# A gated linear-recurrence decoder step on one core: one score matmul per block, two-part sums of squares, and VectorE transposes

## The chip, the cores and the metric

The kernel is one program on one core of a Trainium2 chip. Its inputs are laid out by the host beforehand, and it is launched once. The metric is the device time of one execution in microseconds (us). Before the change three runs took 1477.56, 1477.69 and 1478.64 us, so the median is 1477.69 us.

The engines are named as the profile names them: PE is the matrix engine (PEld its weight loads), DVE is VectorE, ACT is ScalarE, POOL is GpSimd and SP is the engine that issues nearly all DMAs here.

## The reference

264 columns of activations are worked on together: 256 tokens of one prompt and 8 single-token samples. Everything is float32, with a model width of 2048.

```
hx    = rmsnorm(x) ; proj = hx @ w_in            # 11264 outputs: 88 blocks of 128
u     = cg * hc ; a = bg * conv3(u)              # short-convolution branch
f     = lb + (1-lb)*sigmoid(fz) ; log_f = log f ; k = 1-f
b     = cumsum(log_f) inside a chunk of 64 tokens
o     = tril((q e^b) @ (k e^-b)^T) @ v  +  (q e^b) @ S_start       # per head
S_end = e^{b_last} * S_start + (k e^{b_last-b})^T @ v
o     = rmsnorm(o) * silu(og)                    # norm over 128 channels of a head
x     = x + (sig(ga)*(a@w_a) + sig(gb)*(o@w_b)) @ w_out
y     = rmsnorm(x + relu(rmsnorm(x) @ w_up)^2 @ w_down)
```

The prompt's recurrence is exact per token, whatever the chunk length. A sample takes one step of the recurrence with its own stored state, `S = f*S + k v^T`, `o = S^T q`, and returns the new state.

## The kernel before, in words

**Layout.** Channels lie on the 128 partitions and the 264 columns on the free axis. Each large product is made of blocks of 128 output channels. A block's weights (1 MB) come in one DMA (`fetch_w`, L72 to L77). They are split in two halves into a high part `whi` (rounded to fp32r by ACT, L65) and a low remainder `wlo` (DVE, L66). PE adds three fp32r products per tile of 128 input channels, `whi*xh`, `whi*xl` and `wlo*xh` (`gemm`, L90 to L96). A block of 16 tiles is therefore 48 passes over 264 columns.

**Buffers.** There are two raw weight buffers, four buffers for split halves, five PSUM buffers `acc` for the products and three PSUM buffers `mps` for everything small.

**The projection loop** (L538 to L573) has 56 slots, and its order is written out by hand on every engine. In slot i the program first issues the fetch for slot i+2, then evacuates the product of slot i-1 (L508, times `rstd1`), then splits the weights of slot i+1, then runs the steps that are due (`todo`), and then PE does the product of slot i, followed by the small PE work that is due (`todo_pe`). Each engine works through its own instructions strictly in this order. SP's fetch waits until the raw buffer is free, that is until the `wlo` of two slots earlier has been made.

**The recurrence** is done for two heads at a time, a pair; there are four pairs. The 15 steps `s0` to `s14` of a pair (`hgrn`, L252) follow the evacuation of its last block, one per slot. Pairs are evacuated in slots 4, 16, 28 and 40, so step 12 of one pair falls in the slot of step 0 of the next, and step 14 in that of step 2. The steps that matter here:

- `s0` and `s1`: sigmoid and log on ACT (different activation tables, each loaded before use), and `gs`, the 32 columns of factors `f` and `q` for the samples, collected by POOL. PE transposes `gs` at the end of slot 1.
- `s2`: ACT copies the transposed factors to `gsT` (L286), SP writes them to DRAM scratch `scr` (L288), DVE makes the cumulative sum `b`.
- `s3`: SP loads the samples' states `so` and broadcasts the factors from `scr` to all partitions as `fb` and `qb`, six DMAs of 512 KB for a pair (L322 to L324).
- `s4`, `s5`: products with exponentials; PE transposes of `v` and `kend`; ACT copies the transposes to `vk` (L363).
- `sco(i)` (L366 to L382) on PE: for head 0 at the end of slot 5, for head 1 at the end of slot 6. With chunks of 64 inside blocks of 128, it needs two score matmuls within chunks, two 64x64 score matmuls across the two chunks of a block, and two matmuls for the state increments, in two PSUM buffers.
- `s10` to `s13`: squares of `o`, their sum over partitions by a matmul with ones in plain float32 (L433), then log, exp and the products with the gate.

A plain float32 matmul is two passes on PE in the trace; an fp32r one is one.

**The column norms** `rstd1` and `rstd2` sum 16 blocks of squares elementwise, then use three tiny matmuls (`sumsq`), `rstd_diag` on 88x3 values, and a broadcast matmul (L133 to L137). For `rstd1` this is done while PE is in the first product, with the broadcast between its two halves (L551 to L553).

Outside the projection loop the order is set by a scheduler.

## Time and profile before

| what | value |
|---|---|
| median of three runs | 1477.69 us |
| the profiled execution's own time | 1477.44 us |
| its span (first to last instruction) | 1475.7 us |
| granted PE clock, mean | 0.997 |
| PE busy | 1463.1 us, 99% |
| DVE busy | 881.9 us, 60% |
| ACT busy | 707.4 us, 48% |
| POOL busy | 56.5 us, 4% |
| DMA | 285.90 MB, 194 GB/s mean |
| the projection loop with its head | about 29 to 379 us of the span |

The views used are the page with busy times and the chain of waits, the list of groups of instructions, the waits of an engine, the timeline of an engine (start, duration, engine, line, operation, tiles written and read, shapes, count; in brackets the idle time before and what ended it) and the table of windows (busy time of each engine, the granted clock, the share of time in which the 16 DMA engines worked, and GB/s). PE's passes overlap in the records, so what a pass costs is read from the distance between two starts and not from its own duration.

### The profile page before, as it was taken

The page shows a single profiled execution, that of the slowest core. Times are in us where ns is not written, and L with a number is a line of the kernel's source. Part 1 is how long each engine was busy: PE and PEld are TensorE (multiplying, and loading weights), DVE is VectorE, ACT ScalarE, POOL GpSimd, SP SyncE. Part 2 cuts the span into 40 slices and gives each one's busy share as a digit, 9 for nine tenths or more (in the row PEclk, how much of TensorE's full clock was granted, in tenths as well). Part 3 has the DMA queues.
Part 4 walks back from the last instruction along what each step waited for, and adds up shares of the span by engine and source line. Part 5 has one row for each costly group of instructions (what it writes and reads, how often), then busy time and mean ns, then how long its engine had stood idle before and what let it go on. Part 6 is the DMA issues. An engine that isn't in the chain of part 4 may idle for free.

```text
span 1475.7 us, 28089 instructions
## 1 busy us (share of the span) xinstructions
PE 1463.1 (99%) x12158; PEld 1460.0 (99%) x12158; DVE 881.9 (60%) x1154; ACT 707.4 (48%) x953; POOL 56.5 (4%) x87
## 2 busy tenths in 40 slices
PE   9999999999999999999999999999999999999997
PEld 9999999999999999999999999999999999999996
DVE  7667777777655555566655545555455554555554
ACT  7556565665444444444554433444334443344552
POOL 1001011012000000011100000000000000000000
PEclk9999999999999999999999999999999999999998
DMA  7575757575654555555555555455554555545541
GB/s 276 198 256 182 264 187 259 196 260 203 230 195 175 185 187 175 194 197 208 201 172 189 183 177 195 173 190 181 179 193 173 192 179 179 193 173 194 177 171 60
DMA packets 47388, 285.90 MB, mean 194 GB/s; under 512 B 5344, under 2 KB 9200, under 8 KB 16032
## 3 DMA queue, kind: packets, MB, share of 16 engines
q1 hardware_dynamic: 46848, 283.53, 54.1%
q8 instruction: 95, 1.56, 0.4%
q10 hardware_dynamic: 288, 0.40, 0.1%
q14 instruction: 29, 0.24, 0.0%
q0 software_dynamic: 128, 0.19, 0.0%
HBM read 277.07 MB, written 7.02 MB: 193 GB/s over the span
## 4 chain that ended last, share of the span: by engine, by line
PE 98%; DVE 1%; ACT 0%; issue 0%; DVEq 0%; ACTq 0%
PE proj L94 11%; PE proj L95 11%; PE proj L96 11%; PE dn L95 9%; PE up L95 9%; PE up L96 8%; PE dn L96 8%; PE up L94 8%; PE dn L94 8%; PE wo L94 2%; PE wo L95 2%; PE wo L96 2%; PE hd L157 2%; PE wps L112 0%; PE dlps L382 0%; DVE wlo L66 0%
## 5 line engine op out<-in xcount | busy, mean ns | idle before, releaser
L65 ACT CAST whi<-w 128x1024 fp32r<-128x1024 f32 x488 | 508.9, 1048 | 682.6 <-PE dn L95 212.7
L66 DVE TENSOR_TENSOR wlo<-w,whi 128x1024 fp32r<-128x1024 f32 x488 | 597.7, 1234 | 357.4 <-ACT whi L65 355.4
L94 PE MATMUL proj<-xgh,whi 128*128 128x264 f32 x1344 | 384.0, 286 | 0.4 <-DVE q L508 0.4
L95 PE MATMUL proj<-xgl,whi 128*128 128x264 f32 x1344 | 379.4, 282 | 0.0
L96 PE MATMUL proj<-xgh,wlo 128*128 128x264 f32 x1344 | 376.7, 280 | 0.0
L95 PE MATMUL dn<-hl,whi 128*128 128x264 f32 x1024 | 291.8, 285 | 0.0
L95 PE MATMUL up<-x2l,whi 128*128 128x264 f32 x1024 | 291.8, 285 | 0.0
L96 PE MATMUL dn<-hh,wlo 128*128 128x264 f32 x1024 | 289.3, 283 | 0.0
L96 PE MATMUL up<-x2h,wlo 128*128 128x264 f32 x1024 | 289.3, 282 | 0.0
L94 PE MATMUL up<-x2h,whi 128*128 128x264 f32 x1024 | 286.1, 279 | 0.0
L94 PE MATMUL dn<-hh,whi 128*128 128x264 f32 x1024 | 285.8, 279 | 0.0
L94 PEld LDWEIGHTS proj<-xgh,whi 128*128 128x128 f32 x1344 | 251.7, 187 | 0.8 <-ACT whi L65 0.6
L95 PEld LDWEIGHTS proj<-xgl,whi 128*128 128x128 f32 x1344 | 252.2, 188 | 0.2
L96 PEld LDWEIGHTS proj<-xgh,wlo 128*128 128x128 f32 x1344 | 252.3, 188 | 0.0
L94 PEld LDWEIGHTS up<-x2h,whi 128*128 128x128 f32 x1024 | 192.5, 188 | 0.0
L94 PEld LDWEIGHTS dn<-hh,whi 128*128 128x128 f32 x1024 | 192.5, 188 | 0.0
L96 PEld LDWEIGHTS up<-x2h,wlo 128*128 128x128 f32 x1024 | 192.3, 188 | 0.0
L96 PEld LDWEIGHTS dn<-hh,wlo 128*128 128x128 f32 x1024 | 192.3, 188 | 0.0
L95 PEld LDWEIGHTS up<-x2l,whi 128*128 128x128 f32 x1024 | 191.5, 187 | 0.0
L95 PEld LDWEIGHTS dn<-hl,whi 128*128 128x128 f32 x1024 | 191.5, 187 | 0.0
L94 PE MATMUL wo<-mxh,whi 128*128 128x264 f32 x256 | 73.0, 285 | 0.0
L95 PE MATMUL wo<-mxl,whi 128*128 128x264 f32 x256 | 72.3, 283 | 0.0
(405 smaller groups left out, 1304.2 us busy)
## 6 DMA issues: line engine op xcount, KB each, us to landing
w<-in_w_in_dram SPq DMA_DIRECT2D x84, 1024.0 KB, 4.8
w<-in_w_up_dram SPq DMA_DIRECT2D x64, 1024.0 KB, 4.7
w<-in_w_dn_dram SPq DMA_DIRECT2D x64, 1024.0 KB, 4.7
w<-in_w_br_dram SPq DMA_DIRECT2D x16, 1024.0 KB, 4.8
w<-in_w_out_dram SPq DMA_DIRECT2D x16, 1024.0 KB, 4.7
so<-in_shg_dram SPq DMA_DIRECT2D x8, 512.0 KB, 7.4
fb<-scr SPq DMA_DIRECT2D x8, 512.0 KB, 8.3
qb<-scr SPq DMA_DIRECT2D x8, 512.0 KB, 9.4
```

The lines of the kernel that those rows point to most:

```text
L65: nc.scalar.copy(hi, src)
L66: nc.vector.tensor_tensor(lo, src, hi.bitcast(F32), op=ALU.subtract)
L94: nc.tensor.matmul(ps, wh, xh, start=(k == 0), stop=False)
L95: nc.tensor.matmul(ps, wh, xl, start=False, stop=False)
L96: nc.tensor.matmul(ps, wl, xh, start=False, stop=(k == n - 1))
L157: nc.tensor.matmul(hps[i], a[:, i * P:(i + 1) * P], b, start=st, stop=sp)
```

## The change

Five edits go together.

1. **One score matmul per block.** The decay is taken relative to the middle of a block of 128 (`kin`, `qmid`), so one causal matmul of 128x128 covers a block. The two 64x64 matmuls, the ACT copy of their result, and the chunk bookkeeping go. Step 3 has four exponentials still, one of half the size.
2. **Both heads' scores and increments in one place.** `sco(0)` and `sco(1)` both run at the end of slot 5, each in one PSUM buffer, and `sta(0)` and `sta(1)` both in step 6.
3. **Two-part sums of squares.** Squares are split into two fp32r parts and summed by two fp32r matmuls with a 128x128 matrix of ones, which leaves the sum on every partition. For the heads' norms the squares move to steps 9 and 10, the matmuls to the end of step 11, and the steps after them move back by one (`s11` to `s14` run in slots 12 to 15).
4. **The column norms** use the same two matmuls (`rstd_all`), placed after the first product. `rstd` is then computed on 128x264 values, and no broadcast or copy follows. One of the four head accumulators moves from `acc` to `mps`.
5. **Sample factors transposed by VectorE.** Step 1 loses its PE transpose and step 2 its ACT copy; DVE transposes 32x32 blocks, and SP writes them to scratch in four DMAs.

```diff
-    def rstd_diag(ps, n, name):
...
-        r = const.tile([NB, 3], F32, name="r_" + name)
-        nc.vector.tensor_scalar(r, ps[:NB, 0:3], 1.0 / n, EPS, op0=ALU.mult, op1=ALU.add)
+    def ss_parts(ss, name):
+        parts = [tmp.tile([P, T], F32R, tag="t", name=f"{name}_{p}") for p in ("hi", "lo")]
+        split(ss, *parts)
+        return parts
+
+    def rstd_all(parts, n, name):
+
+        ps = mps.tile([P, 512], F32, tag="m", name="ps_" + name)[:, :T]
+        for p in range(2):
+            nc.tensor.matmul(ps, ones_r, parts[p], start=(p == 0), stop=(p == 1))
+        r = const.tile([P, T], F32, tag="rstd", name=name)
+        nc.vector.tensor_scalar(r, ps, 1.0 / n, EPS, op0=ALU.mult, op1=ALU.add)
         nc.vector.reciprocal(r, r)
         nc.scalar.activation(r, r, AF.Sqrt)
...
-    hps = [acc_tile(f"hd{i}") for i in range(4)]
+    hps = [acc_tile(f"hd{i}") for i in range(3)] + [mps.tile([P, 512], F32, tag="m", name="hd3")[:, :T]]
...
-        def s1p():
-            st["gsps"] = mps.tile([P, 512], F32, tag="m", name="gsps")
-            nc.tensor.transpose(out=st["gsps"][:32, :P], in_=st["gs"].rearrange("p a b c -> p (a b c)"),
-                                identity=ident)
-
         def s2():
-            gsT = hp.tile([32, P], F32, tag="gsT", name="gsT")
-            nc.scalar.copy(gsT, st["gsps"][:32, :P])
+
+            gsT = hp.tile([P, 32], F32, tag="gsT", name="gsT")
+            nc.vector.transpose(out=gsT, in_=st["gs"].rearrange("p a b c -> p (a b c)"))
             scr = st["scr"] = dram.tile([2, 2, TS, P], F32, name=f"scr{j}")
-            nc.sync.dma_start(scr.rearrange("a b c d -> (a b c) d"), gsT)
+            for c in range(4):
+                nc.sync.dma_start(scr.rearrange("a b c d -> (a b c) d")[:, 32 * c:32 * c + 32],
+                                  gsT[32 * c:32 * c + 32])
...
+            for dst, at in ((st["kend"], P - 1), (st["kin"], CH - 1)):
+                nc.vector.tensor_tensor(dst, b3[:, :, at:at + 1].broadcast_to([P, 4, P]), b3, op=ALU.subtract)
...
         def sco(i):
             ps = mps.tile([P, 512], F32, tag="m", name="scps")
+            p3 = ps.rearrange("p (a c) -> p a c", c=P)
+            st["scps", i], st["dl", i] = p3[:, 0:2], p3[:, 2:4]
             for blk in range(2):
-                r = slice(blk * P, (blk + 1) * P)
-                qb = qin[:, i, 2 * blk:2 * blk + 2].rearrange("p c l -> p (c l)")
-                nc.tensor.matmul(p3[:, blk], st["kin"][:, i, r], qb, start=(blk == 0), stop=(blk == 1))
+                nc.tensor.matmul(p3[:, blk], st["kin"][:, 2 * i + blk], st["qmid"][:, 2 * i + blk],
+                                 start=(blk == 0), stop=False)
+            vk = st["vk", i]
             for blk in range(2):
-
-                nc.tensor.matmul(p3[:CH, 2, blk * CH:(blk + 1) * CH], kend[:, 2 * i + blk, 0],
-                                 qin[:, i, 2 * blk + 1], start=(blk == 0), stop=(blk == 1))
-            vk = st["vk", i]
-            ps = mps.tile([P, 512], F32, tag="m", name="dlps")
-            dl = st["dl", i] = ps[:, :2 * P].rearrange("p (a c) -> p a c", c=P)
-            for blk in range(2):
-                nc.tensor.matmul(dl[:, blk], vk[:, 2 + blk, :], vk[:, blk, :], start=(blk == 0), stop=(blk == 1))
+                nc.tensor.matmul(p3[:, 2 + blk], vk[:, 2 + blk, :], vk[:, blk, :], start=False, stop=(blk == 1))
...
+        def squares(i):
...
+            nc.scalar.activation(st["sq"][:, i], st["o"][:, i], AF.Square)
+            split(st["sq"][:, i], st["sqh"][:, i], st["sql"][:, i])
...
-                5: (s5, lambda: sco(0)), 6: (s6, lambda: sco(1)), 7: (s7, s7p), 8: (s8, None),
-                9: (s9, None), 10: (s10, s10p), 11: (s11, None), 12: (s12, None), 13: (s13, None), 14: (s14, None)}
+                5: (s5, lambda: (sco(0), sco(1))), 6: (s6, None), 7: (s7, s7p), 8: (s8, None),
+                9: (s9, None), 10: (s10, None), 11: (lambda: None, s10p), 12: (s11, None), 13: (s12, None),
+                14: (s13, None), 15: (s14, None)}
...
-                gemm(ps, wk[i], xg, range(8))
-                nc.scalar.copy(rstd1, rstd_bcast(dg1, "rstd1"))
-                gemm(ps, wk[i], xg, range(8, 16))
+                gemm(ps, wk[i], xg)
+                rstd1 = rstd_all(parts1, 2048, "rstd1")
```

How instructions now stand, at three places. First PE at the end of a slot with step 5 (`scps` are the scores, `vk` the transposed operands of the increments). Before, and after it the same place now:

```order
L96 MATMUL proj<-xgh_426,wlo 128x264
L373 MATMUL scps<-qin,kin 128x128 x2
L376 MATMUL scps<-qin,kend 64x64 x2
L382 MATMUL dlps<-vk_1158 128x128 x2
L94 MATMUL proj<-xgh_147,whi 128x264
```
```order
L96 MATMUL proj<-xgh_428,wlo 128x264
L362 MATMUL scps<-qmid,kin 128x128 x2
L366 MATMUL scps<-vk_1157 128x128 x2
L362 MATMUL scps<-qmid,kin 128x128 x2
L366 MATMUL scps<-vk_1159 128x128 x2
L94 MATMUL proj<-xgh_149,whi 128x264
```

The second head's matmuls came in front of the next product, and the 64x64 ones are gone.

Second ACT, from the logarithm of the first pair's norms to the logarithm of the second pair's gates (`rs` is the norm, `sig` a sigmoid, `lf` the log of the gates). Before, and then now:

```order
L438 ACT_TABLE_LOAD
L438 ACTIVATE rs<-onps,eps 128x264 x2
L65 CAST whi<-w 128x1024 x2
L441 ACT_TABLE_LOAD
L441 ACTIVATE rs<-rs 128x528
L260 ACT_TABLE_LOAD
L260 ACTIVATE sig<-q 128x528
L261 ACTIVATE fz<-fz 128x528
L65 CAST whi<-w 128x1024 x2
L274 ACTIVATE sig<-og 128x528
L277 ACT_TABLE_LOAD
L277 ACTIVATE lf<-fz 128x512
```
```order
L429 ACT_TABLE_LOAD
L429 ACTIVATE rs<-onps,eps 128x264 x2
L259 ACT_TABLE_LOAD
L259 ACTIVATE sig<-q 128x528
L260 ACTIVATE fz<-fz 128x528
L65 CAST whi<-w 128x1024 x2
L432 ACT_TABLE_LOAD
L432 ACTIVATE rs<-rs 128x528
L273 ACT_TABLE_LOAD
L273 ACTIVATE sig<-og 128x528
L276 ACT_TABLE_LOAD
L276 ACTIVATE lf<-fz 128x512
```

The old pair's two norm steps came in one slot later each, beside the new pair's sigmoids, and the sequence has five table loads in place of four.

Third DVE, in the slot of step 2 of the second pair (`b` is the cumulative sum), before and now:

```order
L508 TENSOR_TENSOR cg<-proj,rstd_460 128x264
L66 TENSOR_TENSOR wlo<-w,whi 128x1024 x2
L66 TENSOR_TENSOR ol<-og,oh 128x264 x2
L292 SCALAR_TENSOR_TENSOR b<-smask,lf 128x256 x2
L298 TENSOR_TENSOR kend<-b 128x4x2x64
```
```order
L500 TENSOR_TENSOR cg<-proj,rstd_558 128x264
L66 TENSOR_TENSOR wlo<-w,whi 128x1024 x2
L436 SCALAR_TENSOR_TENSOR og<-og,pt,rs 128x528
L281 STREAM_TRANSPOSE gsT<-gs 128x32
L289 SCALAR_TENSOR_TENSOR b<-smask,lf 128x256 x2
L297 TENSOR_TENSOR kend<-b 128x512
L297 TENSOR_TENSOR kin<-b 128x512
```

and SP there, now (before, one `scr` DMA of 32x128 stood in the place of the four):

```order
L76 DMA w<-in_w_in_dram 128x2048 x5
L284 DMA scr_1814<-gsT 32x32 x4
L76 DMA w<-in_w_in_dram 128x2048
L321 DMA so<-in_shg_dram 128x1024
L322 DMA fb<-scr_1814 128x1024
```

The factors for `scr` now come from DVE behind the weight split of that slot and one product, where they came from ACT ahead of it, and the weight fetch stands behind four DMAs that wait for them.

More of the change, by code (lines that the diff above doesn't have):

```diff
@@ L106, in hybrid_step @@
     nc.vector.memset(ones, 1.0)
+    ones_r = const.tile([P, P], F32R, name="ones_r")
+    nc.gpsimd.tensor_copy(out=ones_r, in_=ones)
     eps = const.tile([P, 1], F32, name="eps")
@@ L120, in sumsq @@
                              start=(start and b == 0), stop=(stop and b == 2))
[L122 to L125 removed]
+    def ss_parts(ss, name):
[8 more added lines that the diff above has]
+        nc.vector.tensor_scalar(r, ps, 1.0 / n, EPS, op0=ALU.mult, op1=ALU.add)
         nc.vector.reciprocal(r, r)
         nc.scalar.activation(r, r, AF.Sqrt)
[L128 to L137 removed]
+        return r
     pt = const.tile([P, N_PAR], F32, name="pt")
@@ new lines, in s3 @@
+            st["qmid"] = wide_home("qmid", "qmid")[:, :2 * TP].rearrange("p (n l) -> p n l", l=P)
+            st["eb"] = wide_home("eb", "eb")[:, :TP].rearrange("p (a l) -> p a l", a=2)
+            nc.scalar.activation(st["kend"], st["kend"], AF.Exp)
+            nc.scalar.activation(st["qmid"], st["kin"], AF.Exp, scale=-1.0)
+            nc.scalar.activation(st["kin"], st["kin"], AF.Exp)
+            nc.scalar.activation(st["eb"], st["b"][:, :, P:], AF.Exp)
+        def s4():
+            kk = st["kk"].rearrange("p a (n l) -> p (a n) l", l=P)
+            qin = st["qin"] = hp.tile([P, 2, P], F32, tag="qin", name="qin")
+            nc.vector.tensor_tensor(st["kend"], st["kend"], kk, op=ALU.mult)
+            nc.vector.tensor_tensor(st["kin"], st["kin"], kk, op=ALU.mult)
+            qmid = st["qmid"].rearrange("p (a n) l -> p a (n l)", a=2)
+            nc.vector.tensor_tensor(qmid, q[:, :, :TP], qmid, op=ALU.mult)
+            nc.vector.tensor_tensor(qin, q[:, :, P:TP], st["eb"], op=ALU.mult)
@@ L355, in s4p @@
                     nc.tensor.transpose(out=p3[:, blk], in_=iv[:, i, r], identity=ident)
-                    nc.tensor.transpose(out=p3[:, 2 + blk], identity=ident,
-                                        in_=st["kend"][:, 2 * i + blk, 1:3].rearrange("p c l -> p (c l)"))
+                    nc.tensor.transpose(out=p3[:, 2 + blk], in_=st["kend"][:, 2 * i + blk], identity=ident)
                 st["trps", i] = p3
@@ L408, in s7p @@
                                      start=(blk == 0), stop=False)
-                nc.tensor.matmul(ps[:, P:2 * P].rearrange("p (c l) -> p c l", l=CH), st["S", i][:, 0],
-                                 st["qin"][:, i, 2:5:2], start=False, stop=True)
+                nc.tensor.matmul(ps[:, P:2 * P], st["S", i][:, 0], st["qin"][:, i], start=False, stop=True)
         def s8():
-            o = st["o"] = pair_tile("o", tag="kin")
+            o = st["o"] = wide_home("o", "kin").rearrange("p (a t) -> p a t", a=2)
             for i in range(2):
@@ L426, in s10 @@
             s_red(1)
[L427 to L428 removed]
+            squares(1)
         def s10p():
@@ L432, in s10p @@
                 ps = st["onps", i] = mps.tile([P, 512], F32, tag="m", name="onps")[:, :T]
-                nc.tensor.matmul(ps, ones, st["sq"][:, i], start=True, stop=True)
+                nc.tensor.matmul(ps, ones_r, st["sqh"][:, i], start=True, stop=False)
+                nc.tensor.matmul(ps, ones_r, st["sql"][:, i], start=False, stop=True)
         def s11():
@@ L645, in hybrid_step @@
             if rstd2 is None:
-                ps2 = mps.tile([P, 512], F32, tag="m", name="ps2")
-                sumsq(ps2, ss2, True, True)
-                rstd2 = const.tile([P, T], F32, tag="rstd", name="rstd2")
-                nc.scalar.copy(rstd2, rstd_bcast(rstd_diag(ps2, 2048, "rstd2"), "rstd2"))
+                rstd2 = rstd_all(parts2, 2048, "rstd2")
             t = t264("h")
```

72 lines of the change are left out of this document (20 added, 52 removed).

## Prediction

> **What bounds the kernel now.** I read the page's busy times first, then its chain of waits, then PE's own waits.
>
> ```profile
> PE 1463.1 (99%) x12158; PEld 1460.0 (99%) x12158; DVE 881.9 (60%) x1154; ACT 707.4 (48%) x953; POOL 56.5 (4%) x87
> PE 98%; DVE 1%; ACT 0%; issue 0%; DVEq 0%; ACTq 0%
> ...
> PE proj L94 <- DVE q L508: 0.4, 1, 0.4
> PE onps L433 <- ACT sq L428: 0.3, 1, 0.3
> ```
>
> PE is busy for 99% of the span and the chain lies on it for 98%. Between the first product and the last it waits only twice for anything, the two rows of waits above. So each pass taken off PE shortens the time by its whole distance to the next pass, and each new wait of PE lengthens it by its whole length. The question is then how many passes go, and what the moved work makes late. A difference under 0.2% (3 us) could not be told from no change here.
>
> **Passes that go.** At the end of a slot with scores PE starts its passes like this (columns: start, duration, engine, line, operation):
>
> ```profile
> 89.52 0.28 PE L96 MATMUL proj<-xgh,wlo 128*128 128x264 f32 x1
> 89.64 0.60 PE L373 MATMUL scps<-qin,kin 128*128 128x128 f32 x4
> ...
> 91.22 0.29 PE L95 MATMUL proj<-xgl,whi 128*128 128x264 f32 x1
> ...
> 104.09 0.61 PE L407 MATMUL ops<-scm,vk 128*128 128x128 f32 x4
> ...
> 104.76 0.61 PE L407 MATMUL ops<-scm,vk 128*128 128x128 f32 x4
> ```
>
> From L96 to the L95 of the next product are 1.70 us; without scores two ordinary steps of 0.12 lie there. One head's block therefore costs 1.46 us, a pair's two 2.92. Now a pair has one block of 16 passes of 128 columns. Six such passes (the state's outputs) take 104.76 - 104.09 = 0.67, so 0.112 each. 16 of them with the same entry and exit (0.12 + 15 x 0.112 + 0.24, less 0.24) cost 1.80. The four pairs gain 4 x 1.12 = **4.5 us**. It could be 4 if the entry into the second head costs a step.
>
> The sums of squares and the transpose of the factors:
>
> ```profile
> 122.72 1.05 PE L433 MATMUL onps<-sq,ones 128*128 128x264 f32 x4
> ...
> 123.73 0.29 PE L95 MATMUL proj<-xgl,whi 128*128 128x264 f32 x1
> ...
> 349.06 1.16 PE L433 MATMUL onps<-sq,ones 128*128 128x264 f32 x4 [0.26 <-ACT sq L428]
> ...
> 65.60 0.27 PE L281 MATMUL gsps<-ident,gs 128*32 128x128 f32 x1
> ...
> 65.83 0.28 PE L95 MATMUL proj<-xgl,whi 128*128 128x264 f32 x1
> ```
>
> The norm's two matmuls hold PE 123.73 - 122.72 - 0.12 = 0.89; four fp32r passes at an ordinary 0.12 are 0.48. That is 4 x 0.41 = **1.6**, and the wait in the last pair goes as its matmul gets another slot, **0.4**. The transpose costs 0.23 - 0.12 = 0.11, four times **0.45**.
>
> **The column norms.** Here a wait goes and another comes. Rows of PE, DVE and ACT, and two groups of DVE (count, busy, mean ns):
>
> ```profile
> 29.46 0.56 PE L119 MATMUL ps<-ones,ss 128*88 128x1 f32 x6
> ...
> 30.08 0.29 PE L95 MATMUL proj<-xgl,whi 128*128 128x264 f32 x1
> ...
> 32.84 0.61 PE L136 MATMUL bps_rstd<-dg_rstd,ones 88*128 88x264 f32 x2
> ...
> 33.41 0.28 PE L95 MATMUL proj<-xgl,whi 128*128 128x264 f32 x1
> ...
> 33.88 1.28 ACT L563 ACT_TABLE_LOAD   x1
> 35.43 0.17 DVE L564 TENSOR_TENSOR lbm<-lbx 128x8 f32<-128x8 f32 x1 [1.08 <-ACT lbx L563]
> 36.15 0.76 DVE L508 TENSOR_TENSOR q<-hd,rstd 128x264 f32<-128x264 f32 x2
> ...
> 36.72 0.36 PE L94 MATMUL proj<-xgh,whi 128*128 128x264 f32 x1 [0.38 <-DVE q L508]
> ...
> L126 DVE RECIPROCAL r_rstd<-r_rstd 88x3 f32<-88x3 f32 x2 | 0.3, 172 | 0.1
> ...
> L565 DVE RECIPROCAL lbm<-lbm 128x8 f32<-128x8 f32 x1 | 0.2, 203 | 0.0
> ```
>
> The tiny sums cost 0.50 (29.46 to 30.08 less 0.12), the broadcast 0.45, and the wait for the first evacuation, which the moved accumulator removes, 0.63 with its ramp. Two passes (0.24) replace them. For `rstd2` that is 0.50 + 0.45 - 0.24 = **0.7**: there the first evacuation may come late, as PE has other accumulators and DVE is 60% busy.
>
> For `rstd1` it is not so. The first product now starts at 29.46, takes 48 x 0.12 = 5.76, and the two passes end the slot at 35.46. Only then does a chain start that before was over by 33.88, and whose values are 264 wide. The reciprocal is the unknown. Its rows rise by 31 ns over 5 elements, 6.3 ns each, which makes 172 + 261 x 6.3 = 1.8 us for 264 by estimate. If it cost what an evacuation costs it would be 0.4; I take 1.8, as the slope is of the operation itself, and 2.3 as the upper end. DVE begins 0.2 after the slot's end (35.66), scale and add 0.4, reciprocal 1.8, square root on ACT 0.4: `rstd1` at 38.3. From the table load to `lbm` are 1.55, from there to the first evacuation 0.72 (rows 33.88, 35.43, 36.15): evacuations start at 40.6. Behind five of them (0.34 each) DVE makes the first half of `wlo` for the third product, in 1.2: 43.5. PE has finished the second product at 41.22 and wants that half two passes later, at 41.46. The new wait is **2.05**, so the head loses 0.24 + 2.05 - 0.50 - 0.45 - 0.63 = **0.7** net (a gain of 0.7 with the short reciprocal).
>
> **What the moved norm steps make late.** The old pair's log now runs in the slot of the new pair's first sigmoids, its exp beside the second. ACT before, from the new pair's step 0 on, then DVE and SP in the slot of step 2, then the arrival two slots later:
>
> ```profile
> 126.26 0.85 ACT L438 ACTIVATE rs<-onps,eps 128x264 f32<-128x264 f32 x2
> ...
> 129.51 1.05 ACT L65 CAST whi<-w 128x1024 fp32r<-128x1024 f32 x1 [1.46 <-PE proj L95]
> 130.58 1.28 ACT L441 ACT_TABLE_LOAD   x1
> 131.88 0.65 ACT L441 ACTIVATE rs<-rs 128x528 f32<-128x528 f32 x1
> ...
> 133.82 0.65 ACT L260 ACTIVATE sig<-q 128x528 f32<-128x528 f32 x1
> ...
> 141.45 2.90 DVE L66 TENSOR_TENSOR wlo<-w,whi 128x1024 fp32r<-128x1024 f32 x2
> 144.26 0.77 DVE L66 TENSOR_TENSOR ol<-og,oh 128x264 fp32r<-128x264 f32 x2
> ...
> 144.37 0.34 SPq L76 DMA_DIRECT2D w<-in_w_in_dram  x1
> ...
> 147.00:155.00 8.00, 8.00 (x69) 8.00 (x68) 6.19 (x11) 6.82 (x10) 0.00 (x0) 1.00 0.99 371
> ...
> 161.34 2.00 ACT L65 CAST whi<-w 128x1024 fp32r<-128x1024 f32 x2 [7.31 <-DMA w<-in_w_in_dram]
> 163.24 1.07 ACT L363 COPY vk<-trps 128x512 f32<-128x512 f32 x2
> ...
> 164.94 0.61 PE L373 MATMUL scps<-qin,kin 128*128 128x128 f32 x4
> ```
>
> After the half split at 129.51, which waits for PE and keeps its place, ACT has five loads of 1.28, the two logs (0.85), two sigmoids, a sigmoid of the gate, an exp and a log (about 0.6 each) and a full split (1.9) before it may start the next weights: it reaches them at 142.8 to 143.0, where before it did at 139.3. The two halves are done at 145.0. DVE's two `wlo` then end at 146.4 to 146.9, not at 144.3; a product (0.7) and the 32x32 transposes follow, for which no row stands: 0.15 (the shortest DVE rows) to 0.45 (an evacuation), I take 0.25. Then SP issues four DMAs, about 0.39 apart as 144.37 and its follower at 144.77 are, and only then the weight fetch: at 149.1. It is **4.75 us late** (4.3 to 5.3).
>
> From that fetch on the DMA engines are full (share 0.99 in the row of windows) with 1 MB, six loads of 512 KB and the next 1 MB, which lands 17.0 us after it (144.37 to 161.34). So it lands as much later. Behind it ACT has the split in two halves and then the first `vk` copy, done at 163.8, now at 168.5. PE wants it after four score passes, at 164.94 + 0.44 - 0.11 = 165.3: a wait of **3.2**. Before there was a cover of 1.5. In the first and third pair the cover is larger:
>
> ```profile
> 87.29 1.06 ACT L363 COPY vk<-trps 128x512 f32<-128x512 f32 x2
> ...
> 238.02 1.06 ACT L363 COPY vk<-trps 128x512 f32<-128x512 f32 x2
> ...
> 240.24 0.60 PE L373 MATMUL scps<-qin,kin 128*128 128x128 f32 x4
> ```
>
> In the third, 238.55 + 4.75 against 240.6 is **2.7**, and I give the fourth the same. The first has no older pair: its fetch is late by the transposes and issues alone, 1.8, and its copy done at 87.85 was wanted at 89.97 (89.64 + 0.33): a cover of 2.1, so no wait. In the last pair DVE gets two more subtractions (0.43) that wait for a square and a cast on ACT (0.4 each), at the place where row 349.06 shows PE already waiting for that chain; I add **0.5** (0 to 1.5). The removed ACT and DVE work of steps 4 and 6 lies beside PE and is worth nothing by itself.
>
> **The sum.** Gains 4.5 + 1.6 + 0.4 + 0.45 + 0.7 = 7.65. Losses 0.7 + 3.2 + 2.7 + 2.7 + 0.5 = 9.8. The profiled execution took 1477.44 (its span and 1.7 around it; 0.25 under the median): 1477.44 - 7.65 + 9.8 = **1479.6 us**. The bounds, reciprocal -1.4 to +0.5, lateness -1.4 to +1.6, last pair -0.5 to +1, give 1476.5 to 1482.5.
>
> **Rivals.** *The fetch is late by SP and the one product alone* (2.4 us), because ACT's load is absorbed: in the slots before, ACT stood idle 1.46 here and 0.65 and 1.21 after. Against it: 3.4 us of work are added and the split at 129.51 cannot start earlier. Waits of 0.9, 0.4 and 0.4 and no tail would give 1477.44 - 7.65 + 0.7 + 1.7 = 1472.2; without any wait there, 1470.5.
>
> *PE's clock falls in the new waits.* PE begins the program slowly:
>
> ```profile
> 1.12 5.28 PE L112 MATMUL wps<-ones 128*128 128x128 f32 x24 [1.12 <-DVE eps L108]
> ```
>
> 24 passes of 128 columns in 5.1 us are 0.213 each, against 0.112 later: half speed after idling. If each of the three waits near 3 us brings that back for as long, it loses 2.5 more: 1479.6 + 7.5 = 1487, slower. It decides from the idle time at which the clock falls; from the first product to the last no idle time reached 1 us before, so the trace is silent on that. The Trainium skill (TensorE: Matmul & The Clock Gate, What's actually happening) puts the fall at about 3.4 us of idleness and the return at about 3.4 us of work; by it the longest wait stands just under the point, and at 1.7 lost per wait the sum would be 1484.7 by estimate. No run here shows it yet.
>
> *A table switch costs more than its load.* The Trainium skill (ScalarE: Activation LUTs, What ACT_TABLE_LOAD costs) counts 1.28 for the load, which the trace agrees with, and about 1.38 of draining on top. Here two loads more a pair would then make the fetch 2.8 later still, by estimate 1488. The trace speaks against it: from the load at 130.58 to the next start at 131.88 are 1.30 in all.
>
> *The change doesn't do what it says* (fp32r sums slower than an ordinary pass, say at the 0.22 of the plain ones): 1.6 and 1 of the gains go, 1482.
>
> **How the numbers follow.** Forecast 0.58 (within its bounds a little more than half lies under 1480.7), fetch less late 0.24, clock 0.12, table 0.01, slow sums 0.05. Faster by over 0.2% is under 1474.7: 0.20, nearly all of the second case. Slower is over 1480.7: 0.24 of the forecast and 0.17 of the last cases, 0.41. The rest, 0.39, can't be told from no change. The range, 1472 to 1485, leaves out the best of the fast case and the clock at its full price.
>
> **What would show it.** Right: PE waits under `vk` or `scps` (ACT copy) of 3 us in the second to fourth pair and not in the first; a PE wait of 2 us at the third product behind `wlo`; RECIPROCAL 128x264 near 1.8; 16 passes of the pair at 0.112; the weight fetch behind `scr` 4 to 5 us later against its slot. Wrong: no wait at `scps`, or a granted clock under 0.99 there.

## The result, and the profile after

| what | before | after |
|---|---|---|
| median of the runs, us | 1477.99 (1477.56 to 1478.88, six) | 1487.63 (1484.56 to 1488.85, six) |
| the profiled execution's own time, us | 1477.44 | 1488.74 |
| its span, us | 1475.7 | 1487.0 |
| granted PE clock, mean | 0.997 | 0.993 |

The changed kernel is **slower by 0.62%**: the ratio is 1.0062, with a 95% interval of 1.0052 to 1.0072. The forecast was 1479.6 us with a range to 1485, so the time lies outside the range. The changed kernel's runs also lie 4.3 us apart, those of before 1.3.

The page after the change shows it first in two rows, PE's busy time and the shares of the chain of waits:

```profile
PE 1461.7 (98%) x12110; PEld 1459.3 (98%) x12110; DVE 886.9 (60%) x1162; ACT 712.8 (48%) x960; POOL 55.0 (4%) x87
...
PE 84%; DMA 5%; DVE 4%; ACT 4%; issue 2%; DVEq 0%; ACTq 0%; SPq 0%; POOLq 0%
```

PE has 48 instructions fewer, but its busy time fell by only 1.4 us and the chain now leaves PE for 16% of the span. Where it leaves shows in PE's own waits (total, count, longest):

```profile
PE scps L366 <- ACT vk L354: 9.2, 4, 3.3
PE proj L96 <- DVE wlo L66: 1.9, 1, 1.9
...
PE br1a L94 <- ACT whi L65: 0.7, 1, 0.7
...
PE br1o L94 <- ACT whi L65: 0.4, 1, 0.4
```

Before there were two waits of 0.4 and 0.3 in that stretch. Now there are 12.2 us of them: at the scores' increments, at the third product, and at the second block of the branches (`br1a`, `br1o`), which the prediction did not have.

That the busy time hardly fell is the second thing. This is PE's timeline at the increments of the second pair (start, duration):

```profile
166.82 0.61 PE L362 MATMUL scps<-qmid,kin 128*128 128x128 f32 x4
170.26 0.71 PE L366 MATMUL scps<-vk 128*128 128x128 f32 x4 [2.84 <-ACT vk L354]
...
171.97 0.42 PE L95 MATMUL proj<-xgl,whi 128*128 128x264 f32 x1
172.19 0.42 PE L96 MATMUL proj<-xgh,wlo 128*128 128x264 f32 x1
172.41 0.42 PE L94 MATMUL proj<-xgh,whi 128*128 128x264 f32 x1
...
174.83 0.40 PE L96 MATMUL proj<-xgh,wlo 128*128 128x264 f32 x1
175.05 0.30 PE L94 MATMUL proj<-xgh,whi 128*128 128x264 f32 x1
175.19 0.28 PE L95 MATMUL proj<-xgl,whi 128*128 128x264 f32 x1
175.31 0.28 PE L96 MATMUL proj<-xgh,wlo 128*128 128x264 f32 x1
```

Behind the wait the passes come 0.22 apart instead of 0.12, until 175.05, and then at the old pace at once. The same stretch stands behind the wait at the third product (15 passes) and behind the one of the fourth pair, but not behind the one of the third pair, although that one took 2.93 us. In windows of 3.41 us (length, busy time and number of instructions of PE, PEld, DVE, ACT and POOL, granted clock, DMA) the clock of these stretches is half. The rows are a window with the wait and the next one for the second pair, the window with the wait of the third pair, and two rows for the fourth pair:

```profile
168.22:171.64 3.42, 1.38 (x13) 1.38 (x13) 2.83 (x5) 2.65 (x5) 0.00 (x0) 1.00 0.13 53
171.64:175.05 3.41, 3.41 (x19) 3.41 (x17) 2.26 (x6) 2.99 (x6) 0.00 (x0) 0.50 0.88 298
...
246.73:250.14 3.41, 1.66 (x14) 1.66 (x15) 3.11 (x6) 2.64 (x6) 0.00 (x0) 1.00 0.02 7
321.82:325.24 3.42, 0.55 (x5) 0.36 (x4) 0.99 (x1) 2.07 (x3) 0.00 (x0) 1.00 0.52 220
325.24:328.65 3.41, 2.95 (x14) 2.96 (x15) 2.55 (x7) 2.64 (x8) 0.00 (x0) 0.50 0.29 60
```

So far the account of the profiled execution, against that of before. The starts of PE's products are 10.85 us later at the end of the projection loop and of the branch weights' wait. Of that are 2.1 the wait at the third product, 9.8 the four waits for `vk` (0.4, 3.0, 2.9, 3.5, from the distance of the starts less one pass), 4.7 the three slow stretches, 1.7 the two waits at the second branch block with the longer first pass behind each; the gains take 8.5 back, as the run with the repairs and the table order shows below, and some 1.0 is noise at the program's start and the first pass after each wait. Then `rstd2` gives 0.7, and 1.1 is lost in the tail: the last norm's broadcast matmuls run at half clock here (0.67), where before the clock fell only behind them, and the last transfers land 0.46 later. This makes 11.3, as the profiled times do (1488.74 - 1477.44).

### The profile page after: what moved, and what is told of

Its sections match the earlier page's. It is cut to its first block, busy times and chain, and to the rows that moved or that the text cites. A ratio compares the mean times of both kernels' runs of the same rounds, so it can differ in the third digit from the quotient of the medians.

```text
span 1487.0 us, 28005 instructions
## 1 busy us (share of the span) xinstructions
PE 1461.7 (98%) x12110; PEld 1459.3 (98%) x12110; DVE 886.9 (60%) x1162; ACT 712.8 (48%) x960; POOL 55.0 (4%) x87
## 3 DMA queue, kind: packets, MB, share of 16 engines
q8 instruction: 94, 1.54, 0.4%
## 4 chain that ended last, share of the span: by engine, by line
PE 84%; DMA 5%; DVE 4%; ACT 4%; issue 2%; DVEq 0%; ACTq 0%; SPq 0%; POOLq 0%
PE dn L94 9%; PE up L94 8%; PE up L95 8%; PE dn L95 8%; PE up L96 8%; PE dn L96 8%; PE proj L96 6%; PE proj L94 6%; PE proj L95 6%; DMA w<-in_w_in_dram 5%; DVE wlo L66 2%; PE wo L96 2%; PE wo L95 2%; PE wo L94 2%; PE hd L158 2%
## 5 line engine op out<-in xcount | busy, mean ns | idle before, releaser
L94 PE MATMUL proj<-xgh,whi 128*128 128x264 f32 x1344 | 381.7, 284 | 0.0
L94 PE MATMUL dn<-hh,whi 128*128 128x264 f32 x1024 | 291.9, 285 | 0.0
L94 PE MATMUL up<-x2h,whi 128*128 128x264 f32 x1024 | 291.8, 285 | 0.0
L96 PE MATMUL up<-x2h,wlo 128*128 128x264 f32 x1024 | 285.7, 279 | 0.0
L96 PE MATMUL dn<-hh,wlo 128*128 128x264 f32 x1024 | 285.7, 279 | 0.0
```

The costliest lines, as they stand in the source:

```text
L94: nc.tensor.matmul(ps, wh, xh, start=(k == 0), stop=False)
L96: nc.tensor.matmul(ps, wl, xh, start=False, stop=(k == n - 1))
```

## The experiments

The theory after this reading: the removed passes gain what was reckoned; the waits for `vk` come from one late weight fetch per pair, through two causes that add (SP standing behind the transpose and its four writes; ACT's moved table loads); the wait at the third product is the `rstd` chain's; the wait at `br1a` comes from a buffer that the last pair's `og` leaves late; and the clock takes about half as much again. The rivals put the waits on ACT alone or SP alone, and the slow passes on something other than idling.

### The transpose a step earlier

```diff
         def s1():
+            gsT = st["gsT"] = hp.tile([P, 32], F32, tag="gsT", name="gsT")
+            nc.vector.transpose(out=gsT, in_=st["gs"].rearrange("p a b c -> p (a b c)"))
             sig = wide_home("sig", "kend").rearrange("p (a t) -> p a t", a=2)
...
         def s2():
-            gsT = hp.tile([P, 32], F32, tag="gsT", name="gsT")
-            nc.vector.transpose(out=gsT, in_=st["gs"].rearrange("p a b c -> p (a b c)"))
+            gsT = st["gsT"]
```

> The changed kernel with VectorE's transpose of the sample factors moved from step 2 to the front of step 1, so that the four writes to scratch in SP's queue find it done; nothing else is moved. Late fetch (theory): the 28.4 us in which SP's queue stood behind the transpose fall to under 4, the waits of the last three pairs' scores for vk (9.2 us in the group of four) fall under 1.5, the slow passes behind two of them (about 3.1 us) go too, and the time is 1487.6 - 9.2 - 3.1 + about 0.7 = 1476. ACT's own order (rival: the vk copies are late since ACT's two table loads stand ahead of them, whatever SP does): the waits stay over 6 us in all, time 1483 or more.

Measured: 1475.87 us (ten runs), ratio to before 0.9984 (0.9975 to 0.9994). The expectation of 1476 held. First the fetch in the changed kernel, on SP, and what SP stood behind:

```profile
148.91 2.00 SPq L284 DMA_DIRECT2D scr<-gsT  x4
151.02 0.35 SPq L76 DMA_DIRECT2D w<-in_w_in_dram  x1
...
SPq L284 <- DVE gsT L281: 28.4, 4, 7.6
```

And with the earlier transpose, SP's timeline and PE's waits:

```profile
140.68 1.97 SPq L284 DMA_DIRECT2D scr<-gsT  x4
147.18 0.35 SPq L76 DMA_DIRECT2D w<-in_w_in_dram  x1
...
PE proj L96 <- DVE wlo L66: 1.9, 1, 1.9
PE scps L366 <- ACT vk L354: 1.4, 2, 0.9
```

In the slot's own time (the fetch's start less that of the slot's first pass; 140.93 before, 142.90 in the changed kernel, 141.77 here) the fetch went out at 3.44 before, at 8.12 after the change, and at 5.41 now: 4.68 late, then 1.97 late. The four writes are now out 4.5 us ahead of the fetch and cost nothing. From the fetch to the wait the way leads over ACT, which stands for the weights and copies `vk` behind their split (in the changed kernel):

```profile
167.74 1.99 ACT L65 CAST whi<-w 128x1024 fp32r<-128x1024 f32 x2 [9.35 <-DMA w<-in_w_in_dram]
169.63 1.07 ACT L354 COPY vk<-trps 128x512 f32<-128x512 f32 x2
```

That split begins 16.72 us after the late fetch of 151.02, and 17.07 after that of 147.18 with the earlier transpose, so the lateness goes through to `vk`. The waits for `vk` fell from 9.2 to 1.4 us, and no slow stretch was left behind them. The rival that ACT's order alone makes them late has fallen.

### lb and oml a slot later

The eight small operations that make `lb` and `oml` go from behind `rstd1` to slot 2, behind that slot's splits:

```diff
             half(i + 1, 1)
+            if i == 2:
+                lbx = const.tile([P, 2, NC_], F32, name="lbx")
...
             if i == 0:
                 gemm(ps, wk[i], xg)
                 rstd1 = rstd_all(parts1, 2048, "rstd1")
-                lbx = const.tile([P, 2, NC_], F32, name="lbx")
```

> The changed kernel with the computation of lb and oml (eight small operations) moved from behind rstd to slot 2, behind that slot's weight splits. Theory: the third product waited 2.1 us for wlo since the first evacuation and the split stood behind these operations on VectorE, and the 15 slow passes behind the wait cost another 1.7; both go: 1487.6 - 3.8 = 1483.8. Rival: the reciprocal of 128x264 (1.80 us) and the wait for TensorE's sums are enough by themselves: the wait stays over 1.2 us, the passes stay slow, 1486.5 or more.

Measured: 1484.57 us, ratio 1.004 (1.0025 to 1.0054). It held: no wait at the third product is in the trace any more, and no slow stretch behind it. (The third pair's wait, too, is followed by a slow stretch in this trace.) DVE in the changed kernel, with the wait for ACT's exponential and its table load in front of the evacuations:

```profile
36.78 1.80 DVE L136 RECIPROCAL rstd<-rstd 128x264 f32<-128x264 f32 x1
...
40.60 0.17 DVE L553 TENSOR_TENSOR lbm<-lbx 128x8 f32<-128x8 f32 x1 [1.72 <-ACT lbx L552]
...
41.32 0.76 DVE L500 TENSOR_TENSOR q<-hd,rstd 128x264 f32<-128x264 f32 x2
```

and with `lb` moved:

```profile
36.18 1.80 DVE L136 RECIPROCAL rstd<-rstd 128x264 f32<-128x264 f32 x1
38.48 0.77 DVE L500 TENSOR_TENSOR q<-hd,rstd 128x264 f32<-128x264 f32 x2 [0.49 <-ACT rstd L137]
```

From the reciprocal's start to the evacuation are 2.3 us instead of 4.5. The eight operations took the other 2.2, 1.72 of it waiting for ACT's table; without them the reciprocal's 1.80 makes nothing wait.

### The last split of og a slot earlier

```diff
-                14: (s13, None), 15: (s14, None)}
+                14: ((lambda: (s13(), s14())) if j == NH2 - 1 else s13, None),
+                15: ((lambda: None) if j == NH2 - 1 else s14, None)}
```

> The changed kernel with the last pair's split of og (step 15) put directly behind its scaling in slot 14; the other pairs as they are. Theory: the fetch of the branch weights needs the memory that og leaves, and went to SP 10 us later than before since og's last reader moved back by one slot; with the split a slot earlier the waits of br1a and br1o (0.7 and 0.4 us, with slow passes 1.7 in all) go: 1487.6 - 1.7 = 1485.9, no wait at br1a over 0.2. Rival: the fetch is late for another reason (SP's order, or the conversion of other memory): both waits stay, 1487.6.

Measured: 1485.69 us, ratio 1.005 (1.0035 to 1.0065), and neither `br1a` nor `br1o` waits. The four runs lie 3.9 us apart, so the time alone does not show the 1.7; the trace does. In the changed kernel SP's second and third fetch of branch weights went out at 385.28, right behind the last `ol` of the last pair (385.18 on DVE), although SP's queue was free from 381.64 on; ACT then stood 4.4 us for their landing:

```profile
381.31 0.33 SPq L76 DMA_DIRECT2D w<-in_w_in_dram  x1
385.28 0.88 SPq L76 DMA_DIRECT2D w<-in_w_br_dram  x2
```

With the split a slot earlier, where the last `ol` is done at 381.7:

```profile
379.23 0.33 SPq L76 DMA_DIRECT2D w<-in_w_in_dram  x1
381.84 0.33 SPq L76 DMA_DIRECT2D w<-in_w_br_dram  x1
```

In the code the second pool of raw weight buffers is opened when the recurrence's pool closes, so it can take its memory, and the fetch follows the last reader of `og` in both traces. That the pools share this memory is read from the code, not measured.

### TensorE kept busy through the waits

```diff
             st["scps", i], st["dl", i] = p3[:, 0:2], p3[:, 2:4]
+            if i == 0 and j > 0:
+                for _ in range(13):
+                    nc.tensor.matmul(p3[:, 0], ones, ones, start=True, stop=True)
...
                 gemm(ps, wk.pop(i), xg)
+            if i == 1:
+                fill = mps.tile([P, 512], F32, tag="m", name="fill")
+                for _ in range(9):
+                    nc.tensor.matmul(fill[:, :P], ones, ones, start=True, stop=True)
```

> The changed kernel with work added that computes nothing: 13 matmuls of 128x128 ones (about 2.9 us) ahead of the scores of the second to the fourth pair, and 9 (about 2.0 us) behind the second product, so that TensorE works where it stood idle; nothing that waits is moved. Clock (theory): the waits at the same places shrink to under 0.5 us because the added work fills them, the weights come no earlier, but the passes behind them take 0.112 to 0.120 us and not 0.220, the granted clock is 0.996 or more, and 1.7 + 1.6 + 1.6 = 4.9 us go: 1482.7, with runs closer together than 4.3 us. Rival (the slow passes do not come from the idle time, for instance from the weights' arrival itself): they stay at 0.220, the clock at 0.993, and the time is 1487.6 or more.

Measured: 1484.12 us (1483.06 to 1485.02), ratio 1.0039 (1.0024 to 1.0054). PE has no slow stretch in the loop, its mean clock is 0.997, and the runs lie 2.0 us apart. The weights come no earlier. The three places where half clock stood before, in windows:

```profile
43.00:48.00 5.00, 4.99 (x42) 4.78 (x41) 4.23 (x5) 0.60 (x1) 0.00 (x0) 1.00 0.48 159
165.00:168.50 3.50, 3.50 (x33) 3.49 (x32) 2.62 (x4) 2.76 (x4) 0.00 (x0) 1.00 0.30 124
321.00:326.00 5.00, 5.00 (x46) 5.00 (x45) 3.96 (x9) 4.23 (x9) 0.88 (x2) 1.00 0.49 177
```

So the slow passes come from PE's idle time, and useless work is a gain of 3.5 us between the medians of four and of six runs. That is 1.4 less than expected; the trace has a new wait of 1.4 in the fourth pair, where PE's transposes wait for `kend` on DVE.

### The norm steps back in place

```diff
-                9: (s9, None), 10: (s10, None), 11: (lambda: None, s10p), 12: (s11, None), 13: (s12, None),
-                14: (s13, None), 15: (s14, None)}
+                9: (s9, None), 10: (s10, s10p), 11: (s11, None), 12: (s12, None),
+                13: (s13, None), 14: (s14, None)}
```

> The changed kernel with the heads' norms back at the steps of the kernel before (sums at the end of step 10, log, exponential, scaling and split in steps 11 to 14); the two-part squares, the transpose by VectorE and all else as changed. Both causes add (theory): the fetch in question was 4.75 us late, some 2 us of it through ACT's moved table loads and logs, the rest through the transpose's place and its four writes; the lateness falls to about 2.6 us, the waits for vk from 9.2 us to 2 to 3, too short for slow passes (2.7 us gone), the late branch weights are gone too (1.7), and the sums now wait about 0.75 us for their squares in three or four pairs: 1487.6 - 6.7 - 2.7 - 1.7 + 2.5 = 1479. Rival (SP's four writes behind the transpose are the whole cause): waits for vk of 8 us or more as after, 1487.6 - 1.7 + 2.5 = 1488.

Measured: 1487.28 us, ratio 1.007 (1.0051 to 1.0088), 8 us above the theory. PE's waits:

```profile
PE onps L423 <- ACT sqh L65: 6.5, 4, 2.3
PE scps L366 <- ACT vk L354: 3.5, 4, 1.5
```

The waits for `vk` did what the theory said (3.5 us, and the fetch of the second pair 2.93 late), so SP's side is not all. But the sums' waits for their squares were sized from the kernel before, where the chain ahead of them is one square; with two parts a cast on ACT and a subtraction on DVE follow, behind other work, and they took 6.5 us and one slow stretch. This and the longer waits for `vk` make up most of the 8 us; the rest is not accounted for. The moved norms have a price, and leaving them has one that is as high.

### The fifth edit alone, and the first two alone

The kernel before with DVE's transpose and the four writes only:

```diff
-        def s1p():
-            st["gsps"] = mps.tile([P, 512], F32, tag="m", name="gsps")
...
-            nc.scalar.copy(gsT, st["gsps"][:32, :P])
+            nc.vector.transpose(out=gsT, in_=st["gs"].rearrange("p a b c -> p (a b c)"))
...
-            nc.sync.dma_start(scr.rearrange("a b c d -> (a b c) d"), gsT)
+            for c in range(4):
+                nc.sync.dma_start(scr.rearrange("a b c d -> (a b c) d")[:, 32 * c:32 * c + 32],
+                                  gsT[32 * c:32 * c + 32])
```

> The kernel before with the fifth edit alone (VectorE's transpose in step 2 and four writes to scratch; PE's transpose and ACT's copy gone). Theory: alone it makes the fetch about 2.6 us late, which the slack ahead of the vk copies nearly holds: waits for vk of 0.5 to 2 us in all, no slow passes, 0.45 us gained at the transposes: 1478.3 + 1.0 = 1479.3. Rival (it is enough by itself): waits over 6 us in all, 1485 or more. Rival (it needs the moved norms to cost anything): no wait, 1477.9.

Measured: 1480.44 us, ratio 1.0017 (1.0007 to 1.0026). PE waits 2.8 us for work of ACT at `dlps`, and none of these waits is followed by slow passes. The fetch is 2.9, 2.7 and 2.7 us late in the last three pairs, the same as in the run with the norms back in place. Alone the edit is a small loss, somewhat larger than the theory's, and both rivals are out.

The kernel before with one score matmul per block and both heads in one place only, with what the steps from `s2` on need for it (one line of the edit is shown; the transpose of the factors, the sums and the norms stay as before):

```diff
-                5: (s5, lambda: sco(0)), 6: (s6, lambda: sco(1)), 7: (s7, s7p), 8: (s8, None),
+                5: (s5, lambda: (sco(0), sco(1))), 6: (s6, None), 7: (s7, s7p), 8: (s8, None),
```

> The kernel before with the first two edits alone: one score matmul per block, both heads' scores and increments at the end of slot 5 and in one step on VectorE; sums of squares, norms, rstd and the transpose of the sample factors as before. Theory: 1.12 us per pair gained and no wait, 1478.3 - 4.5 = 1473.8. Rival: the second head's increments a slot earlier wait for its vk copy by themselves (2 us or more per pair), 1482 or more; or they take back what the scores gain, 1478.

Measured: 1473.68 us, ratio 0.9972 (0.996 to 0.9984). The starts of PE are 4.3 us earlier behind the loop, with no new wait: 1.15 per pair, once the start's 0.3 is taken off. The scores' term stands.

### The three repairs together, and one table order

The first three edits above in one kernel:

> The changed kernel with the three repairs together: transpose of the sample factors at the front of step 1, lb and oml in slot 2, the last pair's split of og in slot 14. Theory: the gains of the change without its new waits: 1475.9 (with the first alone) - 3.8 (third product, with its slow passes) - 0.8 (what was left at the branch weights) = 1471.3; left over are some 1.4 us of waits for vk, too short for slow passes; granted clock 0.997, runs within 1.5 us. Rival: the repairs share their gain (a wait removed comes back at the next place where weights are late), 1474 or more.

Measured: 1472.04 us (1471.48 to 1473.03), ratio 0.996 (0.9946 to 0.9973). The repairs add up. Left are 1.8 us of waits for `vk`, with the fetch still 1.8 to 2.5 late against its slot in the last three pairs. If that is ACT's table loads, their order should remove it:

```diff
         def s1():
...
             nc.scalar.activation(st["lf"], fz[:, :, :TP], AF.Ln)
+            while held:
+                held.pop()()
...
         def s12():
-            nc.scalar.activation(st["rs"], st["rs"], AF.Exp, scale=-0.5)
+            held.append(lambda: nc.scalar.activation(st["rs"], st["rs"], AF.Exp, scale=-0.5))
+            if j == NH2 - 1:
+                held.pop()()
```

> The kernel with the three repairs, and the exponential of a pair's norms (not the last pair's) moved on ACT behind the next pair's sigmoid and log, in the same slot: ACT then has the sigmoid's table already and keeps the exponential's for step 3, two table loads of 1.28 us fewer per pair. Theory (what is left of the late fetch, some 2 us, comes through ACT's table loads): the waits for vk left with the three repairs (gaps of 0.73, 0.54 and 1.37 us) fall under 0.4 us each, 1472.0 - 1.8 = 1470.2. Rival (what is left is SP's four writes or the transfers themselves): waits as they are, 1472.

Measured: **1468.96 us** (1468.70 to 1469.54), ratio 0.994 (0.9928 to 0.9953), faster than both kernels. The chain of waits:

```profile
PE 99%; DVE 0%; ACT 0%; DVEq 0%; issue 0%
```

No wait of PE is left between the program's start and its tail; the fetch is at most 0.55 late. The starts of PE's products are 8.5 us earlier behind the loop and 9.2 behind `rstd2`. These are the gains of the change without its waits. It is 1.2 us better than expected; a wait of 0.3 for `wlo` in the last pair's slots went too, and the rest of this is not accounted for.

The same order in the changed kernel, with nothing repaired:

> The changed kernel with that move of the exponential alone: transpose, lb and oml, and the last split stay as changed. Both causes add (theory): the fetch is some 2 us less late, each of the three large waits for vk (3.0, 2.9, 3.5 us) falls by 1.5 to 2.5 us to some 1 us, too short for slow passes; head and branch weights stay as they are: 1487.6 - 6 - 2.9 = 1478.7. Rival (the place of the transpose in front of the SP writes is all of it): waits over 2.5 us each, 1486 or more.

Measured: 1480.62 us, ratio 1.0018 (1.0008 to 1.0029). The waits for `vk` are 2.8, 1.9 and 1.9 (6.1 in the profile's count) and none of them is followed by slow passes; the fetch is 3.2, 3.2 and 3.7 late instead of 4.7, 4.6 and 5.1. The waits fell by less than the 1.5 to 2.5 us expected in the second pair (0.2) and the third (1.0), and the time is 1.9 us above the theory. ACT's loads are one cause, SP's order the other, and either one taken away brings 7 us or more, here nearly half of it in the clock.

### Which waits slow the clock

The waits that slow PE and those that don't overlap in length: 2.1 us did it at the third product, 2.9 did not in the third pair. Within each run, though, the slow stretches end on one grid: at 48.83, 175.05 and 328.65 in the changed kernel, 37.0 and 45.0 times 3.413 us apart. One step of this grid is called a cell here. Two more runs were made to test that.

> The changed kernel once more, unaltered, to test a rule read off the traces so far: within a run the slow stretches end on one grid of 3.413 us, and a cell of it is slow when TensorE stood idle for more than some 1.9 us of the cell ahead (seen: not slow up to 1.84, slow from 2.04, mixed at 1.91 and 1.95). Grid (theory): the waits are as in the first run (2.1 at the head, about 3.0, 2.9 and 3.5 at the scores), but another set of them may be slow, since the grid lies elsewhere in each run; all slow stretches end within 0.1 us of one grid, and each wait is slow or not by its idle time in one cell, with no exception outside 1.8 to 2.0 us. Rival (the length of the wait decides, or chance): slow stretches off a common grid, or a wait with over 2.0 us in one cell that is not followed by a slow one.

Measured: 1484.44 us (one execution). This time the third product's wait (2.1) has no slow stretch, the second and the fourth pair have one, ending at 172.61 and 326.17 (44.99 cells apart), and the third pair's wait (2.6) has none. In cells of its grid, each pair of rows one cell with a wait in it and the next:

```profile
165.78:169.20 3.42, 1.50 (x13) 1.50 (x14) 2.96 (x5) 2.65 (x5) 0.00 (x0) 1.00 0.14 60
169.20:172.61 3.41, 3.41 (x17) 3.41 (x17) 2.26 (x5) 2.87 (x6) 0.00 (x0) 0.50 0.84 303
240.84:244.25 3.41, 2.30 (x20) 2.11 (x18) 0.11 (x1) 1.18 (x2) 0.00 (x0) 1.00 0.86 363
244.25:247.66 3.41, 2.07 (x18) 2.07 (x19) 3.31 (x6) 2.64 (x6) 0.00 (x0) 1.00 0.17 24
```

The third pair's wait fell across a cell's border, so neither cell was idle for long. All slow stretches of this run lie on one grid, and no cell with over 2.0 us of idle time in the loop was left without one behind it: the rule held.

```diff
             st["scps", i], st["dl", i] = p3[:, 0:2], p3[:, 2:4]
+            if i == 0 and j > 0:
+                for _ in range(6):
+                    nc.tensor.matmul(p3[:, 0], ones, ones, start=True, stop=True)
```

> The changed kernel with 6 matmuls of 128x128 ones (about 1.3 us of work that computes nothing) ahead of the scores of the second to fourth pair, where the run with 13 had filled the waits; the head is as changed. Grid (theory): the waits shrink to about 1.65, 1.6 and 2.2 us; the first two can't put more than 1.85 us of idle time into one cell of 3.413, so no slow passes follow them, the third only if it falls whole into one cell; 2.9 to 4.1 us of slow passes fewer where the three had them: median 1484.5, all slow stretches of the trace on one grid. Rival (any wait of this kind slows the clock in proportion to its length): slow stretches of half the length behind each, 1486 or more.

Measured: 1482.80 us (1481.38 to 1486.57), ratio 1.0031 (1.0018 to 1.0044). The waits were 2.1, 1.6 and 2.4 us, the first 0.5 longer than expected; the profiled execution is the slowest of the six, with slow stretches behind the first and the third, ending at 172.55 and 329.47 (45.97 cells apart). They are of full length, not half, so the rival falls. But 1.3 us of filling was too little to keep the first wait out of the bound.

Windows laid narrowly around the slow stretches give the grid more exactly than the passes do: the granted clock is 0.50 from 45.37 to 48.78, from 171.66 to 175.07 and from 325.26 to 328.67 in the changed kernel, one cell each. So the grid is known also where a run has only one slow stretch. No mixed case is left. The two cells that lie closest to the bound on either side, each with the next one, from the run with the earlier transpose (third product) and from the one with the table order (third pair):

```profile
40.24:43.65 3.41, 1.54 (x13) 1.29 (x11) 3.34 (x10) 3.41 (x4) 0.00 (x0) 1.00 0.00 0
43.65:47.07 3.42, 3.37 (x15) 3.38 (x16) 3.42 (x4) 0.10 (x1) 0.00 (x0) 0.50 0.28 81
...
242.66:246.07 3.41, 1.62 (x15) 1.43 (x14) 2.56 (x4) 2.73 (x4) 0.00 (x0) 1.00 0.03 12
246.07:249.48 3.41, 3.41 (x31) 3.41 (x30) 2.34 (x9) 3.32 (x8) 0.00 (x0) 1.00 0.72 233
```

All fourteen traces together, up to the last norm: where PE was busy for 1.54 us of a cell or less (1.87 idle or more), the next cell ran at half clock in all 16 cases; where it was busy for 1.62 or more, in none, and six cells lie between 1.62 and 2.0. In the tail, cells with 1.74 to 1.99 us were followed by half clock too. Six passes of one column each (`ps_rstd`, 0.63 us in the records) stand in them; without these the tail agrees (at most 1.36 where the clock fell, at least 1.60 where it did not), but what exactly is counted is not shown. A slow cell costs half of its passes, 1.5 to 1.7 us.

## Why the prediction was wrong

**The step that failed is the price of the clock, which the prediction kept as a rival and put at nothing in its sum.** It gave that rival a chance of 0.12 and priced the forecast by the waits' lengths alone. The waits it forecast itself, one of 2 us and three near 3, were enough: the profiled execution lost 4.7 us in the loop by half clock, and without these it would have taken 1484.0, inside the range. The sign of being wrong that the prediction named, a granted clock under 0.99 at the scores, came: 0.50 for one cell behind the second and the fourth pair's wait. Its price was too high for one wait (2.5 against 1.5 to 1.7), it put none on the wait at the head, and it looked for one idle time at which the clock falls. The runs show a bound between 1.79 and 1.87 us of idle time within one cell of 3.41, so that it also hangs on where the wait falls. The first two edits alone, without waits, ran 1473.7; the waits came with the other three.

The prediction called the trace of before silent on the idle time, since no wait reached 1 us in it. That is right from the first product to the last, but not behind them. In its tail the clock fell behind a window in which PE worked for 1.53 us, although the longest single wait there was 0.97:

```profile
1463.56:1466.97 3.41, 1.53 (x12) 1.29 (x12) 0.97 (x4) 0.63 (x2) 0.00 (x0) 1.00 0.00 0
1466.97:1470.38 3.41, 0.00 (x0) 0.00 (x0) 3.41 (x5) 0.00 (x0) 0.00 (x0) 0.50 0.55 216
```

The Trainium skill (TensorE: Matmul & The Clock Gate, What's actually happening) says that the clock follows a free-running window of 3413 ns; the traces agree, with ends 37.0, 45.0, 44.99 and 45.97 such lengths apart. Its table of states asks for a whole idle window. Here a window that was idle for a little over half of its length (1.87 of 3.41 us) was enough, and the measurement decides.

Point by point:

- **Passes that go**: right. 1.15 per pair for the scores against 1.12, 0.42 per pair for the sums against 0.41, and the last pair's wait and `rstd2` (0.72 against 0.7) as reckoned. All gains together measured 9.2 with the repairs; the prediction's, with the head's removed waits and sums that it netted in its 0.7, make 9.0.
- **The head**: right in time and cause, with the price of the clock missing. The reciprocal was an estimate of 1.8:

```profile
L136 DVE RECIPROCAL rstd<-rstd 128x264 f32<-128x264 f32 x2 | 3.6, 1803 | 0.1
...
L281 DVE STREAM_TRANSPOSE gsT<-gs 128x32 f32<-128x32 f32 x4 | 0.8, 203 | 0.0
```

  The wait was 2.1 (forecast 2.05), and 1.6 of slow passes came on top. The transposes took 0.2 where 0.25 was assumed.
- **The late fetch**: right. 4.68, 4.61 and 5.14 us late against 4.75 (4.3 to 5.3), and 1.97 in the first pair against 1.8, with both causes shown: 1.97 is left of 4.68 without SP's, 2.9 without the moved norms, 3.2 with two loads fewer. The first rival, SP and one product alone, fell with that. The waits were 3.0, 2.9 and 3.5 against 3.2, 2.7 and 2.7, and the first pair's cover of 2.1 was 0.4 short.
- **The last pair's 0.5** did not come: the moved square chain was hidden.
- **The end of the loop**: not foreseen, 1.7 us, and so a second term that stood at nothing. The prediction said of a step that moves what it makes late in the next pair, but not that the last pair's `og` is read a slot later and that the branch weights take its memory.
- **Table switch** and **slow fp32r sums**: both out. A load at 140.87 is followed by its sigmoid at 142.16, 1.29 later, and the four passes of the sums from 130.90 on start 0.12 apart. In all the changed kernel has 27 table loads against 24, one more for each pair that has an older one.
- **Small slips in the working**: the reciprocal's slope is 31/5 = 6.2 ns and not 6.3, and the terms given for the bounds make 1476.3 to 1482.7 and not 1476.5 to 1482.5. Nothing hangs on either.

From 1479.6 to the profiled 1488.7 are 9.1: 4.7 clock in the loop, 0.7 clock in the tail (where the grid lay at the last norm; the kernel with the three repairs has it too, with 1.48 us for those matmuls against 0.90 before), 1.7 end of the loop, 1.2 longer waits, 1.1 noise of the start and the last transfers, less 0.5 that did not come and 0.2 of better gains, 8.7 in all; 0.4 is spread over the first passes after the waits.

## What to carry to other kernels

A new wait of TensorE is not paid by its length alone: when a kernel keeps TensorE busy, price each wait of about 2 us or more with a further 1.6 us and a chance (here 16 of the 24 waits from 2.1 us on, in the loops of eight traces). No wait under 2 us in a loop was followed by slow passes in any of these traces, so waits kept shorter than that, also by useless matmuls, cost their own length alone. When a step is moved, follow the queues it passes (SP's fetches behind its DMAs), the tables it makes another engine load, and the memory whose last reader it delays, also at the end of the loop. Small edits then separate the gain from the damage: this change was worth 8.9 us once a transpose, eight small operations, a split and an exponential stood elsewhere.

## What the runs showed of the hardware that was not expected

- In the loop TensorE's granted clock went to 0.50 for one cell of a fixed grid of 3.41 us whenever TensorE had worked for 1.54 us or less in the cell before, and never when it had worked for 1.62 or more. The grid lies elsewhere in each execution, so the same wait cost 1.5 to 1.7 us in one and nothing in the next. The runs of the changed kernel, with four such waits, lie 4.3 us apart; those of before 1.3, and with all repairs 0.8. It is not the number of waits alone: with three of 3.0 us or more, all of them slow in the trace, four runs lay 1.9 apart.
- Six plain 128x128 matmuls ahead of a wait (1.3 us of work) shortened it by 0.9 to 1.3 us, thirteen (2.9 us) removed it. The medians fell by 4.8 and 3.5 us, although each of the two traces has a new wait elsewhere (0.7 and 1.4 us).
- VectorE's reciprocal of 128x264 float32 values took 1.80 us, 6.2 ns for each element beyond the 0.17 of 88x3.
